# Two of four column groups of an output projection as seven block products on token rows, with weight sums made by adding transfers

## The chip, the cores and the metric

The kernel runs on one core of one Trainium2 chip. The metric is the device time of one execution in microseconds. Before the change it is 1609.59 us, the median of three runs (1609.36 to 1610.12). The profile is of one further execution, which took 1609.98 us and whose span from the first to the last instruction is 1608.3 us.

## The reference, cut to what matters

One layer of a decoder trunk: 512 tokens, width 2048, float32. What is computed last, and what the change touches, is the output projection with its gate, the residual and the final norm:

```
def rmsnorm(x, g):
    y = xf * lax.rsqrt(jnp.mean(xf * xf, axis=-1, keepdims=True) + NORM_EPS)
    return y * g
...
merged = jax.nn.sigmoid(g_mla) * y_mla + jax.nn.sigmoid(g_sgu) * y_sgu   # (512, 2048)
x = x + gate[:, None] * (merged @ w_out[l])                              # w_out (2048, 2048)
return rmsnorm(x, final_norm_g)
```

## The kernel before, in words

**Precision.** Every large product is made of float32 values split in two: a high part in the matmul's own 32-bit type (fp32r) and a low part, the rest. A product takes three matmuls, high by high, high by low, low by high (`mm3`, lines 134 to 137). A split is a ScalarE cast for the high part and a VectorE subtraction for the low part, which reads the cast's result (`hilo`, lines 139 to 141, and `Stream.split_to`, lines 105 and 106).

**The weights' stream.** `Stream` holds the list of all weight tiles of the program in the order in which they are used. A tile is 128 rows of 1024 float32, 512 KB, called a granule here. It lands in one of three raw buffers `wraw0` to `wraw2` and is split into one of two pairs, `w0h`/`w0l` or `w1h`/`w1l`. `get(i, ahead)` splits up to granule i + ahead and then asks for as many transfers as raw buffers are free. `load_before` hangs other transfers ahead of a granule's on SyncE's queue.

**The order is the order of the text.** Nothing reorders instructions: each engine takes its own in the order in which the function writes them, and waits at the first whose inputs or buffer are not ready. Work that is to happen beside a granule's matmuls is written behind the split of the next granule. `pend` is a list of such work; `get` runs one entry of it.

**The output projection.** The activations lie as `mh[j]`, `ml[j]`, 16 chunks of 128 channels by 512 tokens. They are the stationary side, 128 tokens at a time, so that tokens come to lie on the partitions of the result; the weights are the moving side, 512 columns wide. The 2048 columns are four groups `cg`. A granule (cg, i) holds chunks 2i and 2i + 1 for 512 columns; `out_granule` (line 1481) runs its 2 x 4 x 3 = 24 matmuls into four PSUM banks, one for each 128 tokens (n). Column group 0 begins inside the last attention head, while the last heads' chunks are still being made (`merge_a`, line 1451); its granules 3 to 7 and the groups 1 and 2 follow in lines 1552 to 1558. Group 3's eight granules are split into buffers of their own during group 2 (`last_tiles`), and its products run at the end token block by token block, the last block in two halves of 256 columns (lines 1564 to 1575), so that rows can be finished one after the other.

**The end of a column group.** `residual` (line 1541) is, for 128 tokens by 512 columns: VectorE multiplies the bank by the gate row (`sig<-ps,gbc`), adds x (`y<-sig,y`), ScalarE squares and sums the row (`sig<-y`, line 1548), and VectorE multiplies by the final gain (`y<-y,gfb`). For groups 0 to 2 it is put on `pend`. When a token block's last columns are in, the row sum gives a square root on ScalarE (line 1579), a reciprocal on VectorE (line 1580), a scaling in four pieces, and four stores.

## Time and profile before

| | |
|---|---|
| time, median of three runs | 1609.59 us |
| time of the profiled execution | 1609.98 us |
| its span | 1608.3 us |
| TensorE busy | 1594.2 us, 99% |
| VectorE busy | 1165.3 us, 72% |
| ScalarE busy | 755.5 us, 47% |
| GpSimd busy | 105.4 us, 7% |
| mean granted TensorE clock | 0.999 |
| first matmul of granule (0, 4) | 1446.73 us |
| last matmul begins | 1599.56 us |

Times in rows are microseconds from the span's start. In a row of the timeline stand start, duration, engine, source line, operation, what it writes and reads, and in brackets how long the engine had been idle and what ended that. A TensorE row's duration reaches beyond the start of the next, since matmuls are pipelined: the distance of the starts is what counts. Names there leave buffer numbers out: `ps` is any PSUM bank, `w0h` the high part of a split weight tile, `gbc` the gate row, `gfb` the final gain, `sig` a scratch tile, `y` the result.

### The profile page before, as it was taken

The page shows a single profiled execution, that of the slowest core. Times are in us where ns is not written, and L with a number is a line of the kernel's source. Part 1 is how long each engine was busy: PE and PEld are TensorE (multiplying, and loading weights), DVE is VectorE, ACT ScalarE, POOL GpSimd, SP SyncE. Part 2 cuts the span into 40 slices and gives each one's busy share as a digit, 9 for nine tenths or more (in the row PEclk, how much of TensorE's full clock was granted, in tenths as well). Part 3 has the DMA queues.
Part 4 walks back from the last instruction along what each step waited for, and adds up shares of the span by engine and source line. Part 5 has one row for each costly group of instructions (what it writes and reads, how often), then busy time and mean ns, then how long its engine had stood idle before and what let it go on. Part 6 is the DMA issues. An engine that isn't in the chain of part 4 may idle for free.

```text
span 1608.3 us, 26988 instructions
## 1 busy us (share of the span) xinstructions
PE 1594.2 (99%) x10760; PEld 1488.5 (93%) x10760; DVE 1165.3 (72%) x1719; ACT 755.5 (47%) x1259; POOL 105.4 (7%) x128
## 2 busy tenths in 40 slices
PE   9999999999999999999999999999999999999997
PEld 8888889999999999999999999999988889888886
DVE  8989679658777777777677777666777888763453
ACT  4443334355545454454465554554655554542322
POOL 0000000001111111111111111112000000000000
PEclk9999999999999999999999999999999999999999
DMA  9988489568899897898887998887422233336422
GB/s 379 354 296 317 171 280 324 170 193 202 219 253 252 226 252 214 233 258 212 231 253 203 250 268 207 238 193 181 162 87 88 82 105 89 90 109 227 136 87 105
DMA packets 122766, 329.64 MB, mean 205 GB/s; under 512 B 14072, under 2 KB 35600, under 8 KB 115856
## 3 DMA queue, kind: packets, MB, share of 16 engines
q1 hardware_dynamic: 104768, 269.72, 48.0%
q0 software_dynamic: 17872, 58.20, 20.8%
q8 instruction: 84, 1.38, 0.3%
q14 instruction: 42, 0.34, 0.1%
HBM read 303.95 MB, written 23.93 MB: 204 GB/s over the span
## 4 chain that ended last, share of the span: by engine, by line
PE 90%; DVE 4%; DMA 2%; ACT 1%; issue 1%; SPq 0%; DVEq 0%; ACTq 0%
PE ps L1267 15%; PE ps L1269 15%; PE ps L1268 15%; PE ps L136 14%; PE ps L137 14%; PE ps L135 14%; PE ps L1429 1%; DVE wada L126 1%; PE ps L1392 1%; PE ps L1393 1%; DVE t L123 1%; DMA wraw<-in_w 1%; DMA lat<-v_d 1%; DVE lat L123 1%; DMA rope_d<-half 0%
## 5 line engine op out<-in xcount | busy, mean ns | idle before, releaser
L106 DVE TENSOR_TENSOR w0l<-wraw,w0h 128x1024 fp32r<-128x1024 f32 (+3 forms) x74 | 78.8, 1066 | 58.8 <-ACT w0h L105 58.5
L105 ACT CAST w1h<-wraw 128x1024 fp32r<-128x1024 f32 (+3 forms) x74 | 63.9, 863 | 118.8 <-PE ps L137 57.7
L1267 PE MATMUL ps<-hh,w0h 128*128 128x256 f32 x416 | 118.5, 285 | 0.9 <-DVE lat L123 0.9
L105 ACT CAST w0h<-wraw 128x1024 fp32r<-128x1024 f32 (+3 forms) x74 | 68.9, 931 | 106.6 <-PE ps L137 66.5
L1269 PE MATMUL ps<-hh,w0l 128*128 128x256 f32 x416 | 117.7, 283 | 0.0
L1268 PE MATMUL ps<-hl,w0h 128*128 128x256 f32 x416 | 117.7, 283 | 0.0
L106 DVE TENSOR_TENSOR w1l<-wraw,w1h 128x1024 fp32r<-128x1024 f32 (+3 forms) x74 | 73.1, 988 | 59.6 <-ACT w1h L105 58.6
L1267 PE MATMUL ps<-hh,w2h 128*128 128x256 f32 x400 | 113.5, 284 | 0.0
L1267 PE MATMUL ps<-hh,w1h 128*128 128x256 f32 x400 | 113.4, 283 | 0.0
L1268 PE MATMUL ps<-hl,w1h 128*128 128x256 f32 x400 | 113.2, 283 | 0.0
L1269 PE MATMUL ps<-hh,w2l 128*128 128x256 f32 x400 | 113.2, 283 | 0.0
L1268 PE MATMUL ps<-hl,w2h 128*128 128x256 f32 x400 | 113.2, 283 | 0.0
L1269 PE MATMUL ps<-hh,w1l 128*128 128x256 f32 x400 | 113.2, 283 | 0.0
L126 DVE SCALAR_TENSOR_TENSOR wada<-wada,cact 128x2048 f32<-128x2048 f32 x47 | 107.1, 2280 | 0.0
L123 DVE TENSOR_TENSOR w2l<-raw,w2h 128x1024 fp32r<-128x1024 f32 x56 | 68.5, 1224 | 39.0 <-ACT w2h L649 38.9
L136 PE MATMUL ps<-w0l,hh 128*128 128x256 f32 (+3 forms) x288 | 92.7, 322 | 0.1
L135 PE MATMUL ps<-w0h,hh 128*128 128x256 f32 (+3 forms) x288 | 92.7, 322 | 0.0
L137 PE MATMUL ps<-w0h,hl 128*128 128x256 f32 (+3 forms) x288 | 92.4, 321 | 0.0
L135 PE MATMUL ps<-hh,w1h 128*128 128x512 f32 x226 | 89.7, 397 | 0.0
L136 PE MATMUL ps<-hl,w1h 128*128 128x512 f32 x226 | 88.3, 391 | 0.8 <-DVE hl L126 0.8
L137 PE MATMUL ps<-hh,w1l 128*128 128x512 f32 x226 | 88.1, 390 | 0.0
L629 POOL DMA_DIRECT2D wraw<-in_wh x67 | 59.2, 939 | 439.8 <-DVE w0l L123 211.7
(350 smaller groups left out, 5400.5 us busy)
## 6 DMA issues: line engine op xcount, KB each, us to landing
raw<-in_wh SPq DMA_DIRECT2D x105, 512.0 KB, 6.9
wada<-in_wada SPq DMA_DIRECT2D x47, 1024.0 KB, 7.4
wraw<-in_wh POOLq DMA_DIRECT2D x67, 512.0 KB, 6.9
wraw<-in_wh SPq DMA_DIRECT2D x45, 512.0 KB, 7.8
raw<-in_wh POOLq DMA_DIRECT2D x42, 512.0 KB, 7.8
wraw<-in_wo SPq DMA_DIRECT2D x32, 512.0 KB, 3.7
half<-in_w SPq DMA_DIRECT2D x35, 256.0 KB, 5.4
wraw<-in_w SPq DMA_DIRECT2D x16, 512.0 KB, 8.9
```

The costliest lines, as they stand in the source:

```text
L105: self.nc.scalar.copy(hi[:, :n], raw[:, :n])
L106: self.nc.vector.tensor_tensor(out=lo[:, :n], in0=raw[:, :n], in1=hi[:, :n].bitcast(F32), op=ALU.subtract)
L123: DVE.tensor_tensor(out=out, in0=in0, in1=in1, op=op)
L126: DVE.scalar_tensor_tensor(out=out, in0=in0, scalar=scalar, in1=in1, op0=op0, op1=op1, **kw)
L135: PE.matmul(ps, ah, bh, start=start, stop=False)
L136: PE.matmul(ps, ah, bl, start=False, stop=False)
L137: PE.matmul(ps, al, bh, start=False, stop=stop)
L629: q_.dma_start(t, wh[h, n, q // 10 - 1], **eng)
L1267: PE.matmul(ps, wH[:, sl], xh, start=st, stop=False, skip_group_check=True)
L1268: PE.matmul(ps, wH[:, sl], xl, start=False, stop=False, skip_group_check=True)
L1269: PE.matmul(ps, wL[:, sl], xh, start=False, stop=sp, skip_group_check=True)
L1392: PE.matmul(ps, q2[:, q], krh[:, :n], start=False, stop=False)
```

## The change

Column groups 0 and 3 stay as they were, one after the other, and come first. Groups 1 and 2 together become one 2 x 2 block product by Strassen's scheme (in the form with seven products). The blocks on the activations' side are the two halves of the tokens (`left` 0 to 255, `right` 256 to 511) by the two halves of the channels (chunks c and c + 8). On the weights' side they are the two halves of the channels by the two column groups; block 12 is first channels, column group 2.

- **Sums of activations.** `make_dsum(c)`, for c = 0 to 7, forms three sums of 128 x 256 and splits each (five VectorE operations, three casts, three subtractions). It is written behind the granules (0, 4) to (0, 7) and (3, 0) to (3, 3). `make_third(c)` forms a fourth sum over the right half of chunk c in place (two VectorE operations, one split), behind the granules of the products 1 and 7.
- **Sums of weights.** Four tiles `chain[i]` are loaded with block 11, and GpSimd's queue adds to them by adding transfers: block 12 (for product 6), block 22 (for product 2), block 21 (for product 4). Product 3's tiles are loaded with block 12 into a raw buffer, and block 22 is added to the same buffer by a transfer. The products 1, 7 and 5 use a block as it is.
- **Products.** In the order 6, 1, 7, 2, 5, 3, 4, each in four granules (p, i) of 2 chunks x 2 token blocks x 3 = 12 matmuls of 512 columns. The split of the next granule is written ahead of each granule, the work in `tasks` behind it. Product 4 comes last, one token block whole and one in two halves of 256 columns, from buffers of its own.
- **After the products.** `after(p, n2)` copies or combines banks into y, multiplies by the gate, and adds x by an adding transfer; `left_rows` finishes the 256 left tokens during product 4.

The output's tile `y` is split into `y0`, `y3` and two tiles that take over the buffers of the first sums (`s1h`, `s1l`).

**ScalarE, where the first results of the direct column groups are worked off.** Before, column group 1 (the casts of granules (1, 1) to (1, 4) with the squares of group 0 between them):

```order
L105 CAST w0h_131_16183<-wraw1_131_16091 128x1024
L1548 ACTIVATE sig_2083_16192,ssy_2076_16021<-y_2075_16020 128x512
L105 CAST w1h_132_16219<-wraw2_132_16122 128x1024
L1548 ACTIVATE sig_2085_16228,ssy_2076_16021<-y_2075_16020 128x512
L105 CAST w0h_133_16255<-wraw0_133_16153 128x1024
```

Now, column group 3 (the casts of granules (3, 1) to (3, 3); `s1h`, `s2h`, `s4h` are the high parts of the three sums):

```order
L105 CAST w0h_131_16248<-wraw1_131_16117 128x1024
L1554 ACTIVATE sig_2102_16260,ssy_2087_16032<-y0_2081_16026 128x512
L140 CAST s1h_2073_16018<-sig_2104_16288 128x256
L140 CAST s2h_2075_16020<-sig_2103_16287 128x256
L140 CAST s4h_2077_16022<-sig_2104_16288 128x256
L105 CAST w1h_132_16300<-wraw2_132_16161 128x1024
L1554 ACTIVATE sig_2106_16312,ssy_2087_16032<-y0_2081_16026 128x512
L140 CAST s1h_2073_16018<-sig_2108_16340 128x256
L140 CAST s2h_2075_16020<-sig_2107_16339 128x256
L140 CAST s4h_2077_16022<-sig_2108_16340 128x256
L105 CAST w0h_133_16352<-wraw0_133_16205 128x1024
```

Between a square and the next granule's cast stand three more casts, whose inputs VectorE makes behind the residual's last multiplication.

**VectorE, the same place.** Before, from the subtraction of granule (1, 1) to that of (1, 2):

```order
L106 TENSOR_TENSOR w0l_131_16184<-wraw1_131_16091,w0h_131_16183 128x1024
L123 TENSOR_TENSOR sig_2082_16189<-ps0_2052_15864,gbc_2073_16018 128x512
L123 TENSOR_TENSOR y_2075_16020<-sig_2082_16189,y_2075_16020 128x512
L123 TENSOR_TENSOR y_2075_16020<-y_2075_16020,gfb_2074_16019 128x512
L106 TENSOR_TENSOR w1l_132_16220<-wraw2_132_16122,w1h_132_16219 128x1024
```

Now, from that of granule (3, 1); the rows end with the three low parts, and the subtraction of (3, 2) comes next:

```order
L106 TENSOR_TENSOR w0l_131_16249<-wraw1_131_16117,w0h_131_16248 128x1024
L123 TENSOR_TENSOR sig_2101_16257<-ps0_2052_15864,gbc_2079_16024 128x512
L123 TENSOR_TENSOR y0_2081_16026<-sig_2101_16257,y0_2081_16026 128x512
L123 TENSOR_TENSOR y0_2081_16026<-y0_2081_16026,gfb_2080_16025 128x512
L123 TENSOR_TENSOR sig_2103_16287<-b4_1718_13905,g4_1719_13906 128x512
L123 TENSOR_TENSOR sig_2104_16288<-b12_1992_15513,g12_1993_15514 128x512
L123 TENSOR_TENSOR sig_2104_16288<-sig_2103_16287,sig_2104_16288 128x256
L123 TENSOR_TENSOR sig_2103_16287<-sig_2104_16288,sig_2103_16287 128x256
L123 TENSOR_TENSOR sig_2104_16288<-sig_2104_16288,sig_2103_16287 128x256
L123 TENSOR_TENSOR s1l_2074_16019<-sig_2104_16288,s1h_2073_16018 128x256
L123 TENSOR_TENSOR s2l_2076_16021<-sig_2103_16287,s2h_2075_16020 128x256
L123 TENSOR_TENSOR s4l_2078_16023<-sig_2104_16288,s4h_2077_16022 128x256
```

Eight operations have come between the residual and the next granule's subtraction.

**ScalarE in the block products,** which have no counterpart before: the casts of granules (6, 2), (6, 3), (1, 0), (1, 1) and (1, 2). `raw` is a chain tile, `y3` column group 3, `b0` the high part of the fourth sum, and the rows of line 1673 copy product 6 out of its bank:

```order
L140 CAST w1h_2128_16596<-raw2_2085_16030 128x1024
L1554 ACTIVATE sig_2131_16615,ssy_2087_16032<-y3_2082_16027 128x512
L140 CAST w0h_2132_16618<-raw3_2086_16031 128x1024
L1554 ACTIVATE sig_2135_16637,ssy_2087_16032<-y3_2082_16027 128x512
L140 CAST w1h_2136_16641<-wraw2_2117_16562 128x1024
L1554 ACTIVATE sig_2140_16662,ssy_2087_16032<-y3_2082_16027 128x512
L140 CAST w0h_2145_16672<-wraw0_2118_16564 128x1024
L140 CAST b0_1582_13103<-sig_2148_16690 128x256
L1673 COPY s1l_2142_16669<-ps0_2122_16572 128x512
L140 CAST w1h_2149_16696<-wraw1_2119_16566 128x1024
```

Between two casts there now lies one granule of 12 matmuls, where it was one of 24.

**The diff, cut to its core:**

```diff
     go = {}
-    for cg in range(3):
+    for cg in (0, 3):
         for i in range(8):
             go[cg, i] = ws.add(wo[cg, i], GW)
...
+    def w_block(q, i):
+        return wo[q % 10, (q // 10 - 1) * 4 + i]
+    def chain_load(i, q):
+        if q == 11:
+            DMA.dma_start(chain[i], w_block(q, i))
+        else:
+            nc.gpsimd.dma_start(chain[i], w_block(q, i), accum_op=ALU.add)
...
+    def make_dsum(c):
+        a, b = (nt(tp, [P, S], F32, "sig", bufs=3) for _ in range(2))
+        tt(a, mh[c].bitcast(F32), ml[c].bitcast(F32), ALU.add)
+        tt(b, mh[c + 8].bitcast(F32), ml[c + 8].bitcast(F32), ALU.add)
+        tt(b[:, right], a[:, right], b[:, right], ALU.subtract)
+        tt(a[:, left], b[:, right], a[:, left], ALU.subtract)
+        tt(b[:, left], b[:, left], a[:, left], ALU.add)
+        for n, src in (("s1", b[:, right]), ("s2", a[:, left]), ("s4", b[:, left])):
+            hilo(dsum[n + "h"][:, c], dsum[n + "l"][:, c], src)
+    def make_third(c):
+        a = nt(tp, [P, S], F32, "sig", bufs=3)
+        tt(a, mh[c].bitcast(F32), ml[c].bitcast(F32), ALU.add)
+        tt(a[:, left], a[:, left], a[:, right], ALU.subtract)
+        hilo(mh[c][:, right], ml[c][:, right], a[:, left])
+    todo = [lambda c=c: make_dsum(c) for c in range(8)]
+    for cg in (0, 3):
+        if cg:
+            pso = [bank_at(4 + k) for k in range(NB)]
+        for i in range(0 if cg else 3, 8):
+            out_granule(cg, i, pso, 0 if (cg, i) == (3, 7) else 1)
+            if (cg, i) > (0, 3) and todo:
+                todo.pop(0)()
         for n in range(NB):
-            pend.append(lambda n=n, cg=cg, ps=pso[n]: residual(n, cg, slice(cg * 512, (cg + 1) * 512), ps))
-    wl = [get(go[3, i], 0) for i in range(8)]
+            pend.append(lambda n=n, cg=cg, ps=pso[n]: residual(n, cg and 1, columns(cg), yt[cg][:, n], ps))
+    seven = (6, 1, 7, 2, 5, 3, 4)
+    block_of = {1: 11, 7: 22, 5: 21, 3: 12}
...
+    def take(p, i):
+        raw_of[p, i] = t = nt(wp, [P, GW], F32, f"wraw{n_raw[0] % 3}")
+        n_raw[0] += 1
+        DMA.dma_start(t, w_block(block_of[p], i))
+        if p == 3:
+            nc.gpsimd.dma_start(t, w_block(22, i), accum_op=ALU.add)
...
+    def add_x(half, n2, col):
+        n = 2 * half + n2
+        nc.gpsimd.dma_start(y_of(col, half, n2), xn[n][:, columns(col)], accum_op=ALU.add)
+    def after(p, n2):
+        b = banks_of(p)[n2]
+        if p == 6:
+            ACT.copy(y_of(2, 1, n2), b)
...
+        elif p == 3:
+            gated(y_of(1, 1, n2), b, 1)
+            add_x(1, n2, 1)
+            y = y_of(2, 1, n2)
+            tt(y, y, b, ALU.subtract)
+            gated(y, y, 2)
+            add_x(1, n2, 2)
...
+    for s, (p, i) in enumerate(steps):
+        if s == 0:
+            split_step(p, i)
...
+        if p == 4:
+            break
+        if steps[s + 1][0] != 4:
+            split_step(*steps[s + 1])
+            if steps[s + 1] in stream and n_take < len(stream):
+                take(*stream[n_take])
+                n_take += 1
+        granule(p, i, banks_of(p), (0, 1))
+        for f in (pend[:1] if p == 6 else []) + tasks.pop((p, i), []):
+            f()
```

More of the change, by code (lines that the diff above doesn't have):

```diff
@@ new lines, in norm_of, with finish_row @@
+    def norm_of(col, half, n2):
+        norm_part(2 * half + n2, 2 if half else col + 1, columns(col), y_of(col, half, n2), False)
+    def finish_row(n, r, pieces):
+        for k, (cols, y, kind) in enumerate(pieces):
+            if kind == "last":
+                stt(y, y, r, gfb[:, cols], ALU.mult, ALU.mult)
+            elif kind == "act":
+                ACT.activation(y, y, AF.Copy, scale=r)
+            else:
+                ts(y, y, r, None, ALU.mult)
+            DMA.dma_start(out[n][:, cols], y)
```

187 lines of the change are left out of this document (137 added, 50 removed).

## The prediction, made before the changed kernel was run

> **What bounds the kernel now.** I read the page first: who is busy, and whose work ended last.
>
> ```profile
> span 1608.3 us, 26988 instructions
> PE 1594.2 (99%) x10760; PEld 1488.5 (93%) x10760; DVE 1165.3 (72%) x1719; ACT 755.5 (47%) x1259; POOL 105.4 (7%) x128
> PE 90%; DVE 4%; DMA 2%; ACT 1%; issue 1%; SPq 0%; DVEq 0%; ACTq 0%
> ```
>
> TensorE bounds the whole program, so matmuls saved are time saved, as long as TensorE is fed. Next I looked at the busy time of each engine in the stage that changes (us, PE, PEld, DVE, ACT, POOL, granted clock, DMA share, GB/s).
>
> ```profile
> 1450.00:1500.00 50.00, 50.00 (x223) 41.39 (x221) 18.97 (x21) 12.38 (x17) 0.00 (x0) 1.00 0.53 186
> 1500.00:1550.00 50.00, 50.00 (x222) 41.42 (x221) 25.94 (x27) 18.16 (x23) 0.00 (x0) 1.00 0.48 156
> ```
>
> TensorE has no gap there, and VectorE and ScalarE have half their time free. By shares alone there is room. Whether it is usable is decided by the handover of one granule, which the timeline shows.
>
> ```profile
> 1452.17 0.39 PE L135 MATMUL ps<-w0h,b 128*128 128x512 f32 x1
> 1452.37 1.05 ACT L105 CAST w1h<-wraw 128x1024 fp32r<-128x1024 f32 x1 [4.34 <-PE ps L137]
> 1453.46 1.22 DVE L106 TENSOR_TENSOR w1l<-wraw,w1h 128x1024 fp32r<-128x1024 f32 x1 [4.17 <-ACT w1h L105]
> 1457.61 0.39 PE L135 MATMUL ps<-w1h,b 128*128 128x512 f32 x1
> ```
>
> A granule of 24 matmuls takes 1457.61 - 1452.17 = 5.44 us. The cast for the next one starts 0.20 us after the boundary, since only then is its buffer pair free; the subtraction starts 1.09 us after the cast and ends at +2.51. So there are 2.9 us of slack. In the block products a granule is half as long, 2.72 us, and the slack is 0.2 us (0.4 counting that the low part is first used by the second matmul).
>
> **What the change removes.** Column groups 1 and 2 were 2 x 8 granules, now 6 x 4 halves of one and product 4. Full-width matmuls go from 720 to 696, those of 256 columns (the last token block's) from 96 to 48. The halves' pitch comes from these two rows, 48 matmuls apart:
>
> ```profile
> 1594.12 0.42 DVE L123 TENSOR_TENSOR sig<-ps,gbc 128x256 f32<-128x256 f32 x1 [1.47 <-PE ps L137]
> 1599.88 0.42 DVE L123 TENSOR_TENSOR sig<-ps,gbc 128x256 f32<-128x256 f32 x1 [3.61 <-PE ps L137]
> ```
>
> 24 x 5.44/24 + 48 x 5.76/48 = 5.4 + 5.8 = **11.2 us less**, if TensorE stays fed.
>
> **What it adds: chains through two engines.** ScalarE takes its instructions in written order, so a cast queued behind a square or another cast waits for what that one waits for. The residual of 128 x 512 shows the chain:
>
> ```profile
> 1555.73 1.05 ACT L105 CAST w0h<-wraw 128x1024 fp32r<-128x1024 f32 x1 [4.38 <-PE ps L137]
> 1556.82 1.23 DVE L106 TENSOR_TENSOR w0l<-wraw,w0h 128x1024 fp32r<-128x1024 f32 x1 [4.22 <-ACT w0h L105]
> 1557.96 0.68 DVE L123 TENSOR_TENSOR sig<-ps,gbc 128x512 f32<-128x512 f32 x1
> 1558.68 0.69 DVE L123 TENSOR_TENSOR y<-sig,y 128x512 f32<-128x512 f32 x1
> 1559.40 0.63 ACT L1548 ACTIVATE sig<-y 128x512 f32<-128x512 f32 x1 [2.62 <-DVE y L123]
> 1559.94 0.19 ACT L1548 ACTIVATION_READ_ACCUMULATOR sig<-y 128x1 f32 x1
> 1560.16 0.69 DVE L123 TENSOR_TENSOR y<-y,gfb 128x512 f32<-128x512 f32 x1 [0.79 <-ACT sig L1548]
> 1560.77 0.68 DVE L123 TENSOR_TENSOR sig<-ps,gbc 128x512 f32<-128x512 f32 x1
> ```
>
> From the cast's start to the square's end, when ScalarE can take the next cast: 1560.13 - 1555.73 = 4.40 us. Beside granules of 5.44 us that is hidden. The sums' pieces are seen in the earlier projection, which makes the like:
>
> ```profile
> 224.83 1.28 DVE L123 TENSOR_TENSOR t<-hh,hl 128x512 f32<-128x512 f32 x2
> 226.03 0.41 DVE L123 TENSOR_TENSOR lat<-t 128x256 f32<-128x256 f32 x1
> 226.37 0.88 DVE L123 TENSOR_TENSOR t<-t,t 128x256 f32<-128x256 f32 x2
> 227.28 0.42 DVE L123 TENSOR_TENSOR lat<-t,t 128x256 f32<-128x256 f32 x1
> L140 ACT CAST s2h<-t 128x256 fp32r<-128x256 f32 x8 | 3.3, 408 | 0.3
> 1411.36 1.77 ACT L140 CAST lat<-ps 128x512 fp32r<-128x512 f32 x3
> 1413.02 0.59 ACT L140 CAST hh<-ps 128x512 fp32r<-128x512 f32 x1
> ```
>
> So 512 columns take VectorE 0.60 (0.72 when the operation needs the one before it), 256 columns 0.46 in a dependent row; ScalarE takes 0.37 (0.41 less the overlap) for 256 and 0.55 for 512 out of a bank.
>
> *Column group 0, granules 4 to 7.* Split plus `make_dsum`: 1.09 + 1.14 + 0.60 + 0.72 + 3 x 0.46 + 0.37 = 5.30 us until ScalarE is free. Under 5.44: hidden, cost nothing; 0.2 us more on each step would show.
>
> *Column group 3, granules 0 to 3.* The residual of group 0 stands in between: cast to cast is 1.09 + 1.14 + 1.44 (to the square) + 0.76 (square to last multiplication) + 0.61 + 0.60 + 0.72 + 3 x 0.46 + 0.37 = 8.1 us. Four of these from +0.2 put the fifth cast at 32.7; TensorE can start that granule 2.13 us later (subtraction's end less one matmul's pitch), at 34.8 instead of 5 x 5.44 = 27.2. **+7.6 us**; the slack of the first granule is in it.
>
> *Products 6, 1, 7.* Behind each of the four granules of product 6 hangs a residual of group 3: 4.40 us a step. Behind each of product 1 and 7 hangs `make_third`, 1.09 + 1.14 + 0.72 + 0.46 + 0.37 = 3.78 us, with a bank's copy behind it in half of them, 4.33 us. Against 2.72. The cast chain runs 0.2 + 4 x 4.40 + 4 x 4.33 + 4 x 3.78 = 50.2, so granule (2, 1) starts at 52.4 instead of 13 x 2.72 = 35.4: **+17.0 us**. Product 2 has nothing behind it (2.51 us against 2.72), so nothing is made up either.
>
> *Products 5 and 3.* VectorE has two splits in some steps, by the same rows 0.5 us in product 5 and 0.9 in product 3. The larger part is the transfers:
>
> ```profile
> DMA  9988489568899897898887998887422233336422
> wraw<-in_wh POOLq DMA_DIRECT2D x67, 512.0 KB, 6.9
> wraw<-in_wo SPq DMA_DIRECT2D x32, 512.0 KB, 3.7
> DMA to landing us min/median/max: 5.3/6.9/10.7
> DMA to landing us min/median/max: 2.5/4.3/11.8
> ```
>
> The first line is the busy share of the DMA engines in 40 slices of the span. The fourth is the adding transfers' (GpSimd queue), the fifth that of SyncE's loads. The products load 52 tiles of 512 KB where 32 were loaded, 10.5 MB more over some 150 us or 70 GB/s, which the share of 0.5 has room for; what counts is how long one takes to land. A tile of product 3 needs a load and then an adding transfer into the same buffer: 2.5 + 5.3 = 7.8 us at best, 3.7 + 6.9 = 10.6 at the medians. The buffer for (3, 0) comes free when (5, 1) is split, 2.5 us into product 5; its cast is due 8.9 us in. That leaves 6.4, so 1.4 to 4.2 are missing, less 0.3 that the cast had in hand: 1.1 to 3.9. (3, 1) and (3, 2) have used the delay; the buffer of (3, 3) frees when the delayed (3, 0) is split, and the same 1.1 to 3.9 come again. Together 1.4 + 2.2 to 7.8 = 3.6 to 9.2. The adding transfers of before ran where the DMA share was 0.8 to 0.9 (slices 10 to 28), fuller than here, which speaks for the low end; here several are asked for at once, which speaks for the high end. I take the middle, **+6.4 us**. On GpSimd's queue the additions of x stand behind the waiting ones of product 3, and on SyncE's the first stores behind the last load; neither is due before. The adding transfers into `chain` have 8 us and more of lead and cost nothing; if that cover went, their 6.9 would hold ScalarE, behind which all casts stand.
>
> [...]
>
> *The tail.* Before, a token block's chain is seen alone:
>
> ```profile
> 1588.37 0.69 DVE L123 TENSOR_TENSOR sig<-ps,gbc 128x512 f32<-128x512 f32 x1 [6.35 <-PE ps L137]
> 1591.91 0.74 DVE L126 SCALAR_TENSOR_TENSOR y<-y,ry,gfb 128x512 f32<-128x512 f32 x1
> 1594.58 0.43 DVE L123 TENSOR_TENSOR y<-sig,y 128x256 f32<-128x256 f32 x1
> 1596.12 0.15 DVE L132 TENSOR_SCALAR ry<-ry 128x1 f32<-128x1 f32 x1
> 1602.66 0.48 DVE L126 SCALAR_TENSOR_TENSOR y<-y,ry,gfb 128x256 f32<-128x256 f32 x1
> ```
>
> The last matmul is done about 1599.85 and the last operation at 1603.14: 3.3 us. Now product 4 lasts only 5.44 + 2 x 2.88 = 11.2 us, and VectorE does in that time, in order and only after product 3 (+0.2): six operations of `after(3)` (3.9 us), two `left_rows` with a square and a multiplication each (two copies, a square and the multiplication behind a root, about 3.4 us each by the same kind of rows), a block's chain (1592.65 - 1588.37 = 4.3, and 0.3 for its sum), the first half's (1596.27 - 1594.12 = 2.2) and the last (3.3). Sum 20.8 us, or 9.5 after TensorE's end instead of 3.3: 6.2 more; with the adding transfers of x landing 6 us after they are asked for, about 2 more. **+7.2 us** (6.2 to 8.2). The stores behind are as before.
>
> **Sum.** -11.2 + 7.6 + 17.0 + 6.4 + 7.2 = +27.0 us on the profiled execution's 1609.98 (its span is 1608.3, 1.7 us lie around it), so 1637.0; the median of the runs is 0.4 lower, so **1636.6 us**. About 0.2% is what a measurement of this kernel can tell from no change.
>
> **Rivals.**
> 1. *Only busy time counts, the handovers overlap: faster.* The shares of 1450 to 1550 speak for it; the 0.79 us that VectorE idles for the square in the residual's rows, and the order of the casts, speak against. Then column group 3 has 1.14 + 2.05 + 3.65 = 6.84 us of VectorE a granule (+2.5 after slack), product 6 has 3.19 (+1.5), the products 1 and 7 fit, and the tail and the transfers are hidden: -11.2 + 4.0 = -7.2, 1602.4 us. It decides from the point where a cast-to-cast chain is under 2.72 us. Chance 0.05.
> 2. *Adding transfers land like loads,* 3.7 us: each of the two delays is 0.7, the term is 2.8 instead of 6.4, 1633 us. For it: the DMA share is 0.5 here and was fuller where the 6.9 were taken. Against: 5.3 at the least. [...] Chance 0.12.
> 3. *Adding transfers land like the slowest,* 10.7 us: two delays of 7.7, the term is 16.8, 1647 us. For it: several of them at once with loads of the products. Chance 0.07.
> 4. *TensorE's clock falls in the gaps,* 1.6 us in every 4.3. The windows show it granted in full wherever matmuls run, and less only where there are none:
>
> ```profile
> 1590.00:1596.00 6.00, 6.00 (x53) 6.00 (x52) 2.97 (x8) 2.08 (x6) 0.00 (x0) 1.00 0.49 175
> 1600.00:1608.00 8.00, 0.00 (x0) 0.00 (x0) 2.17 (x6) 1.92 (x5) 0.00 (x0) 0.75 0.37 131
> ```
>
> At half clock a granule of the products takes 5.44, more than any chain: 13 x 5.44 = 70.7 instead of 52.4, 18.3 more, 1655 us. [...] Chance 0.08.
>
> **Numbers.** The forecast has 0.66, rivals 0.05, 0.12, 0.07 and 0.08, and 0.02 stay for no change. Range: the low ends of the last two terms give 1632.8, their high ends 1640.4; sixteen chain steps (four of 8.1, twelve in the products) priced 0.35 us too long or 0.4 too short, the size of the handovers in them, give 1627 and 1647. That holds rivals 2 and 3 and leaves out 1 and 4. Faster 0.05, same 0.02, slower 0.93.
>
> **What would show it.** In the changed profile: TensorE idle from granule (3, 2) on, ended by VectorE's low parts; casts 8.1 us apart in column group 3, 4.4 in product 6, 4.3 or 3.8 in 1 and 7, 2.7 in 2; casts of (3, 0) and (3, 3) waiting for an adding transfer; some 10 us between the last matmul and the last operation. Wrong, if casts stand 2.7 us apart in product 6, or TensorE's clock is below 1.00 there, or the end follows the last matmul by 4 us.

## The result, and the profile after

The changed kernel takes 1644.74 us (median of five runs, 1642.78 to 1646.35); the kernel before, beside it, 1609.59 us (five runs, 1608.82 to 1611.01). The ratio is 1.0218, with a 95% interval of 1.0203 to 1.0233: slower, 8 us above the forecast of 1636.6 and inside its range. The profiled execution took 1644.1 us with a span of 1642.3, 34.0 longer than before's.

Its page, first the lines on who is busy and the granted clock, then (with packets, MB and the share of 16 engines) the two large DMA queues. `q1` carries the plain transfers, `q0` the adding ones.

```profile
span 1642.3 us, 27103 instructions
PE 1598.1 (97%) x10688; PEld 1480.0 (90%) x10688; DVE 1219.4 (74%) x1819; ACT 783.6 (48%) x1311; POOL 125.0 (8%) x152
PEclk9999999999999999999999999999999999999997
q1 hardware_dynamic: 106064, 269.72, 47.1%
q0 software_dynamic: 21328, 68.69, 24.0%
```

VectorE and ScalarE are hardly busier than before (74 and 48% for 72 and 47%), yet the kernel lost 34 us: the loss is waiting. The stages show where it is (us, PE, PEld, DVE, ACT, POOL, granted clock, DMA share, GB/s):

```profile
1468.00:1505.00 37.00, 31.01 (x128) 23.97 (x127) 29.79 (x52) 13.66 (x27) 1.70 (x2) 0.98 0.65 172
1521.00:1540.00 19.00, 15.80 (x61) 10.86 (x59) 13.66 (x17) 7.67 (x13) 2.54 (x3) 1.00 0.72 131
1575.00:1590.00 15.00, 14.66 (x64) 11.70 (x63) 10.54 (x11) 8.06 (x9) 2.56 (x3) 1.00 0.91 209
1590.00:1605.00 15.00, 10.96 (x33) 7.27 (x32) 6.36 (x7) 3.99 (x4) 4.27 (x5) 0.77 0.99 209
```

In column group 3 (first row) and product 6 (second row) TensorE has holes while the DMA engines have room. In the products 2 and 5 (third row) it is fed. In product 3 (fourth row) it stands still for over a quarter of the time, VectorE is busy for 6.36 of 15 us, and the DMA engines are full, though they move only 209 GB/s.

**Column group 3.** ScalarE's casts of two successive granules, the square and the first sum's cast between them:

```profile
1476.31 1.05 ACT L105 CAST w1h<-wraw 128x1024 fp32r<-128x1024 f32 x1
1480.03 0.63 ACT L1554 ACTIVATE sig<-y 128x512 f32<-128x512 f32 x1 [2.67 <-DVE y L123]
1483.17 0.41 ACT L140 CAST s1h<-sig 128x256 fp32r<-128x256 f32 x1 [2.42 <-DVE sig L123]
1484.40 1.04 ACT L105 CAST w0h<-wraw 128x1024 fp32r<-128x1024 f32 x1
```

The next granule's cast comes 8.09 us after the last, as the prediction had it (8.1), and 5.1 of these are ScalarE's waits for VectorE, ahead of a cast whose own input has long been there.

**Product 6,** the same engine:

```profile
1520.97 1.05 ACT L140 CAST w0h<-raw 128x1024 fp32r<-128x1024 f32 x1 [4.39 <-PE ps L137]
1524.63 0.63 ACT L1554 ACTIVATE sig<-y 128x512 f32<-128x512 f32 x1 [2.62 <-DVE y L123]
1525.26 1.03 ACT L140 CAST w1h<-raw 128x1024 fp32r<-128x1024 f32 x1
```

4.29 us from cast to cast (predicted 4.40). Behind the granules of the products 1 and 7 they stand 4.19 us apart where a bank's copy follows and 3.71 where none does, in product 2 2.80.

**Product 3.** Its four casts, and the two later ones of its adding transfers on GpSimd's queue:

```profile
1593.78 1.04 ACT L140 CAST w1h<-wraw 128x1024 fp32r<-128x1024 f32 x1 [5.75 <-DMA wraw<-in_wo]
1599.94 1.04 ACT L140 CAST w0h<-wraw 128x1024 fp32r<-128x1024 f32 x1 [4.17 <-DMA wraw<-in_wo]
1605.61 1.04 ACT L140 CAST w1h<-wraw 128x1024 fp32r<-128x1024 f32 x1 [3.66 <-DMA wraw<-in_wo]
1608.41 1.05 ACT L140 CAST w0h<-wraw 128x1024 fp32r<-128x1024 f32 x1 [1.76 <-DMA wraw<-in_wo]
```
```profile
1599.11 0.85 POOL L1610 DMA_DIRECT2D wraw<-in_wo  x1 [7.10 <-issue]
1602.97 0.84 POOL L1610 DMA_DIRECT2D wraw<-in_wo  x1 [3.00 <-DVE s1h L123]
```

All four wait for their tile, not two of them. The tiles of the third and fourth row land 6.5 and 5.4 us after the adding transfer is asked for.

**The tail.** The last matmul, a wait for x, and the last operation:

```profile
1626.20 0.27 PE L1640 MATMUL ps<-s4h,g 128*128 128x256 f32 x1
```
```profile
1622.39 0.63 ACT L1554 ACTIVATE sig<-s1l 128x512 f32<-128x512 f32 x1 [1.35 <-DMA s1l<-in_xn]
1636.39 0.48 DVE L126 SCALAR_TENSOR_TENSOR s1l<-s1l,ry,gfb 128x256 f32<-128x256 f32 x1
```

10.4 us lie between them (1636.87 - 1626.47), where there were 3.3.

**The loss by stages.** First matmuls in the changed kernel: granule (3, 0) of column group 3 at 1467.96, (6, 0) at 1520.77, (2, 2) at 1574.73, product 4 at 1614.95. Fully fed, these stretches would take 8 x 5.44 = 43.5, 14 x 2.72 = 38.1 and 10 x 2.72 = 27.2 us. So 9.3, 15.9 and 13.0 us are lost, and 10.4 - 3.3 = 7.1 in the tail: 45.3, less the 11.2 of saved matmuls, is 34.1, where the spans differ by 34.0. The same subtraction, made on each experiment below (the tail up to the last operation of any engine):

| kernel | time, us | column group 3 | products 6, 1, 7 | products 2 (from its third granule), 5, 3 | tail over before's 3.3 |
|---|---|---|---|---|---|
| changed | 1644.7 | 9.3 | 15.9 | 13.0 | 7.1 |
| late halves | 1622.4 | 1.3 | 1.5 | 13.1 | 7.7 |
| no addition in product 3 | 1633.9 | 7.7 | 15.9 | 1.5 | 10.3 |
| no x | 1640.4 | 9.3 | 15.9 | 10.7 | 4.9 |
| sums later | 1636.1 | 0.0 | 16.0 | 12.9 | 7.5 |
| longer lead | 1620.0 | 0.0 | 2.2 | 9.9 | 9.4 |
| early x | 1617.0 | 0.0 | 2.1 | 9.9 | 6.5 |
| other tail | 1613.8 | 0.0 | 2.1 | 9.8 | 2.4 |
| adding queue | 1611.4 | 0.0 | 2.1 | 7.8 | 2.4 |
| splits later | 1614.3 | 0.0 | 2.1 | 9.7 | 3.1 |
| both | 1611.6 | 0.0 | 2.1 | 7.2 | 1.5 |
| sums on GpSimd | 1626.2 | 0.0 | 11.4 | 9.4 | 2.8 |
| sums on VectorE | 1606.1 | 0.0 | 2.0 | 3.7 | 1.4 |

Where nothing waits, ten granules of the column of the products 6, 1, 7 and two of the next take 2.81 us instead of 2.72: those whose activations are one of the first three sums. That is 0.9 and 0.2 us that no wait makes.

### The profile page after: what moved, and what is told of

Same layout as the page of the kernel before. It is cut to its first block, busy times and chain, and to the rows that moved or that the text cites. A ratio compares the mean times of both kernels' runs of the same rounds, so it can differ in the third digit from the quotient of the medians.

```text
span 1642.3 us, 27103 instructions
## 1 busy us (share of the span) xinstructions
PE 1598.1 (97%) x10688; PEld 1480.0 (90%) x10688; DVE 1219.4 (74%) x1819; ACT 783.6 (48%) x1311; POOL 125.0 (8%) x152
## 3 DMA queue, kind: packets, MB, share of 16 engines
q1 hardware_dynamic: 106064, 269.72, 47.1%
q0 software_dynamic: 21328, 68.69, 24.0%
## 5 line engine op out<-in xcount | busy, mean ns | idle before, releaser
L105 ACT CAST w0h<-wraw 128x1024 fp32r<-128x1024 f32 (+3 forms) x69 | 63.6, 922 | 87.5 <-PE ps L137 48.9
L106 DVE TENSOR_TENSOR w0l<-wraw,w0h 128x1024 fp32r<-128x1024 f32 (+3 forms) x69 | 72.7, 1054 | 41.4 <-ACT w0h L105 41.0
L105 ACT CAST w1h<-wraw 128x1024 fp32r<-128x1024 f32 (+3 forms) x69 | 58.5, 848 | 91.2 <-PE ps L137 35.9
L123 DVE TENSOR_TENSOR w1l<-wraw,w1h 128x1024 fp32r<-128x1024 f32 x51 | 62.4, 1224 | 48.4 <-ACT w1h L638 37.2
L123 DVE TENSOR_TENSOR w0l<-wraw,w0h 128x1024 fp32r<-128x1024 f32 x51 | 62.4, 1224 | 45.9 <-ACT w0h L638 37.5
L106 DVE TENSOR_TENSOR w1l<-wraw,w1h 128x1024 fp32r<-128x1024 f32 (+3 forms) x69 | 67.0, 971 | 34.7 <-ACT w1h L105 33.7
```

Of the source, the lines that this page charges most:

```text
L105: self.nc.scalar.copy(hi[:, :n], raw[:, :n])
L106: self.nc.vector.tensor_tensor(out=lo[:, :n], in0=raw[:, :n], in1=hi[:, :n].bitcast(F32), op=ALU.subtract)
L123: DVE.tensor_tensor(out=out, in0=in0, in1=in1, op=op)
```

## The experiments

The theory after the result had four parts: the order in ScalarE's queue makes the loss in column group 3 and in the products 6, 1, 7; load and adding transfer, on DMA engines that are full, the loss in the products 5 and 3; VectorE's serial work with the waits for x the tail; and a drop of TensorE's clock (0.77 granted from 1590 to 1605 us) adds a little. Rival causes stand in each expectation.

**Late halves: the same instructions in another order.**

```diff
         tt(y, t, y, ALU.add)
-        norm_part(n, part, cols, y, last)
+        later.append(lambda: norm_part(n, part, cols, y, last))
...
-            hilo(dsum[n + "h"][:, c], dsum[n + "l"][:, c], src)
+            later.append(lambda n=n, src=src: hilo(dsum[n + "h"][:, c], dsum[n + "l"][:, c], src))
...
-        hilo(mh[c][:, right], ml[c][:, right], a[:, left])
+        later.append(lambda: hilo(mh[c][:, right], ml[c][:, right], a[:, left]))
...
+        flush()
         granule(p, i, banks_of(p), (0, 1))
```

`flush` runs and empties the list `later`; in column group 3 it stands in `get`, behind the split.

> The same instructions in another order: the second half of every piece of side work (the residual's square and multiplication by the final gain, the casts and low parts of the sums of activations) is written one granule later, behind the next granule's split. Theory (the order in ScalarE's queue makes the stalls): casts stand 5.44 us apart in column group 3 up to what VectorE's 6.84 us of work a step adds, and 2.7 to 3.2 apart in the products 6, 1 and 7; the stall of column group 3 goes from 9.3 to about 3 us, that of the products 6, 1, 7 from 15.9 to about 3; the stall by the transfers of product 3 (13.0) and the tail (7.0) stay: about 1625 us (1622 to 1631). Rival (the amount of work on VectorE and ScalarE makes them): nothing changes, 1643 to 1646 us.

1622.4 us (median of 4; ratio to before 1.0084, 1.0067 to 1.0100). The same 27103 instructions, 22 us less. ScalarE in product 6 now:

```profile
1514.07 1.05 ACT L140 CAST w1h<-raw 128x1024 fp32r<-128x1024 f32 x1 [1.76 <-PE ps L1648]
1515.03 0.62 ACT L1562 ACTIVATE sig<-y 128x512 f32<-128x512 f32 x1
1516.93 1.05 ACT L140 CAST w0h<-raw 128x1024 fp32r<-128x1024 f32 x1 [1.19 <-issue]
1518.34 0.63 ACT L1562 ACTIVATE sig<-y 128x512 f32<-128x512 f32 x1 [0.36 <-DVE y L123]
```

The first square no longer waits, the second for 0.36 us instead of 2.62, and the casts stand 2.86 us apart. Column group 3 took 1511.07 - 1466.22 = 44.9 us, the products up to (2, 2) 1550.63 - 1511.07 = 39.6. So the order, not the amount of work, made 22.4 of the 25.2 us that column group 3 and the products 6, 1, 7 had lost.

**No addition in product 3.**

```diff
     DMA.dma_start(t, w_block(block_of[p], i))
-    if p == 3:
-        nc.gpsimd.dma_start(t, w_block(22, i), accum_op=ALU.add)
```

> Product 3's weights stay block 12: the adding transfers of block 22 are left out, everything else is as in the changed kernel. Theory (load and adding transfer one after the other, on crowded DMA engines, delay the splits of product 3): the stall of the products 5 and 3 goes from 13.0 to 2 to 4 us, 1634 us (1632 to 1637). Rival (VectorE's and ScalarE's double splits in these products make it): it stays at 11 or more, 1643 us.

1633.9 us, one run. Product 4 starts 1601.49 - 1572.75 = 28.7 us after (2, 2). The casts of product 3 wait for TensorE again and no longer for a tile:

```profile
1590.18 1.05 ACT L140 CAST w0h<-wraw 128x1024 fp32r<-128x1024 f32 x1 [1.42 <-PE ps L1638]
1592.85 1.06 ACT L140 CAST w1h<-wraw 128x1024 fp32r<-128x1024 f32 x1 [0.66 <-PE ps L1638]
1595.57 1.05 ACT L140 CAST w0h<-wraw 128x1024 fp32r<-128x1024 f32 x1 [1.66 <-PE ps L1638]
```

Of the 13.0 us, 11.5 hang on the four adding transfers. Of the 1.5 that stay, 1.3 are the double splits, which the prediction had at 1.4. The tail has grown by 3.2: its work starts earlier, and three of its squares wait 3.11, 2.03 and 0.79 us for x.

**No x.**

```diff
     n = 2 * half + n2
-    nc.gpsimd.dma_start(y_of(col, half, n2), xn[n][:, columns(col)], accum_op=ALU.add)
```

> The eight adding transfers of x into column groups 1 and 2 are left out (x is missing there), the rest as in the changed kernel. Theory (the DMA engines are full while product 3's weights are fetched, and x's 1 MB in that stretch is part of it): the delay of product 3 shrinks by 2 to 5 us, and the tail by 1 to 2, 1639 us (1637 to 1642). Rival (each transfer's own latency makes the delay, whatever else moves): product 3's stall stays at 12 to 13, the tail loses 0 to 1, 1643 to 1645 us.

1640.4 us, one run. From (2, 2) to product 4 1613.40 - 1575.54 = 37.9 us, 10.7 lost instead of 13.0, and the tail 4.9 instead of 7.1. Both moved as expected of full engines, but x's transfers are the small part.

**Sums later.**

```diff
-            if (cg, i) > (0, 3) and todo:
+            if i > 3 and todo:
                 todo.pop(0)()
```

> The last four sums of activations are written behind the granules 4 to 7 of column group 3, where no residual stands, instead of 0 to 3. Theory (a step of residual plus sums takes ScalarE's queue 8.1 us, one of them alone 4.4 or 5.3): the stall of column group 3 goes from 9.3 to 0 to 1 us, with the dip of the clock in it, and the rest stays, 1635.5 us (1634 to 1638). Rival (the stall belongs to the sums themselves, wherever they stand): 1643 to 1646 us.

1636.1 us, one run. Column group 3 takes 1512.28 - 1468.76 = 43.5 us, nothing lost. The sums cost nothing where no residual stands beside them; the collision of the two did.

**Longer lead.** The two orders together, and:

```diff
-    n_raw, n_part = [ws.next_raw], [ws.next_part]
+    n_raw, n_part = [0], [ws.next_part]
+    rings = [(wp, f"wraw{(ws.next_raw + q) % 3}") for q in range(3)] + [(dp[0].p, f"ex{q}") for q in range(2)]
...
-    while n_take < 3:
+    while n_take < len(rings):
```

> The late second halves and the later sums together, and two more raw buffers for the products' weights, so that product 3's loads and adding transfers are asked for five tiles ahead instead of three. Theory (product 3's stall is the time of load plus adding transfer on crowded DMA engines against too short a lead): the stall of the products 5 and 3 goes from 13.1 to 2 to 6 us, the tail stays at 7 to 8: about 1611 us (1608 to 1615). Rival (the DMA engines have no room at all there, so that asking earlier only moves the crowd): the stall stays at 10 or more, 1618 to 1621 us.

1620.0 us (4 runs; 1.0058, 1.0042 to 1.0075). My theory missed here: the stall went only to 9.9, and the rival's time came. What is late now is not product 3's tile but the chain's, for product 4, on ScalarE:

```profile
1573.28 1.04 ACT L140 CAST s2h<-raw 128x1024 fp32r<-128x1024 f32 x1 [7.35 <-DMA raw<-in_wo]
1574.23 1.04 ACT L140 CAST w1h<-wraw 128x1024 fp32r<-128x1024 f32 x1
```

That cast is not due before product 4 and holds the one behind it. The chain's additions were asked for late, since one of product 3's stood ahead of them on GpSimd's queue and waited 12.42 us there:

```profile
1563.08 0.85 POOL L1619 DMA_DIRECT2D ex<-in_wo  x1 [12.42 <-DVE s1h L123]
1563.62 2.94 POOL L1547 DMA_DIRECT2D raw<-in_wo  x3
```

So two more causes were possible, the two queues, beside full engines.

**Early x.**

```diff
         if p == 6:
-            ACT.copy(y_of(2, 1, n2), b)
+            gated(y_of(2, 1, n2), b, 2)
+            add_x(1, n2, 2)
         elif p == 1:
-            ACT.copy(y_of(1, 0, n2), b)
+            gated(y_of(1, 0, n2), b, 1)
+            add_x(0, n2, 1)
...
+        task(1, 2 + n2, lambda n2: DMA.dma_start(y_of(1, 1, n2), xn[2 + n2][:, columns(1)]), n2)
```

> As with the longer lead, and x goes earlier: the copies of product 6 and product 1 are gated at once and x is added to them then, the right tokens' column group 1 gets x by plain loads, and four of the fourth sums move to product 2. Only two of eight adding transfers of x stay where they were. Theory (the transfers of x crowd product 3's and hold the tail's squares): the stall of the products 5 and 3 goes to 1 to 4 us, the tail to 5 to 6, though VectorE gets two more operations there: about 1608 us (1605 to 1612). Rival (the tail is VectorE's serial work alone): tail 8 to 9, no gain over the longer lead alone, 1611 us.

1617.0 us (4 runs; 1.0041, 1.0026 to 1.0056), above both expectations, since the stall stays at 9.9. The tail is 6.5, between the two, instead of 9.4, with two VectorE operations more, so the waits for x had held it: none of its squares waits for x any longer.

**Other tail.**

```diff
-            tt(y, y, gfb[:, cols], ALU.mult)
+            (eng or DVE).tensor_tensor(out=y, in0=y, in1=gfb[:, cols], op=ALU.mult)
...
-        norm_part(2 * half + n2, 2 if half else col + 1, columns(col), y_of(col, half, n2), False)
+        norm_part(2 * half + n2, 2 if half else col + 1, columns(col), y_of(col, half, n2), False, nc.gpsimd if half else None)
...
-                          for cg, k in ((0, "act"), (1, "act"), (2, "dve"), (3, "dve"))])
+                              for cg, k in ((0, "act"), (1, "act"), (2, "pool"), (3, "pool"))])
```

> As with the early x, and in the tail some of VectorE's work goes to GpSimd and ScalarE: the multiplication of the right tokens' column group 2 by the final gain, half of the scaling of the left rows, and one piece of each last row; both left blocks' sums, roots and reciprocals are written side by side. Theory (VectorE's 22 us of serial work behind product 3 against 11 us of product 4 make the tail): about 5 us of VectorE's work less, tail 2 to 4 us over before's, 1604 us (1601 to 1608). Rival (GpSimd and VectorE hold each other up, or the adding transfers still set the end): tail at 5 or more, 1607 to 1611 us.

1613.8 us (10 runs; 1.0025, 1.0016 to 1.0035). The tail came as expected (2.4). The time fits neither expectation, since both had counted on a smaller stall, and it is still 9.8.

**Adding queue, splits later, both.** The first writes product 3's additions one granule behind their loads, the second moves product 4's splits back, the third does both and orders the tail's VectorE work anew:

```diff
-            nc.gpsimd.dma_start(t, w_block(22, i), accum_op=ALU.add)
+            adds.append(lambda: nc.gpsimd.dma_start(t, w_block(22, i), accum_op=ALU.add))
...
-    for i, at_ in enumerate(((5, 1), (5, 2), (5, 3), (3, 0))):
+    for i, at_ in enumerate(((5, 3), (3, 0), (3, 1), (3, 2))):
```

> As the kernel with the other tail, with one thing changed: product 3's adding transfers are written one granule after their loads, so that the chain's additions of block 21 do not stand behind them in GpSimd's queue. Theory (the first of product 3's adding transfers waits 10 us for its own load and holds the three additions into the chain behind it, for which ScalarE's early casts of product 4's weights wait): those three are asked for about 8 us earlier, and the stall of the products 5 and 3 goes from 9.8 to 2 to 5 us, 1608 us (1606 to 1611). Rival (the DMA engines are full there, whatever the order): the stall stays at 8 or more, 1612 to 1615 us.

> As the kernel with the other tail, with one thing changed: product 4's splits stand two granules later, so that their casts wait less for the chain's additions and hold the products' casts behind them less. Theory (a cast that is not due yet waits in ScalarE's queue ahead of one that is): the wait of 8.0 us for the chain's second tile shrinks by two granules, 5.4 us, and the stall of the products 5 and 3 goes from 9.8 to 3 to 6 us, 1609 us (1607 to 1612). Rival (full DMA engines: product 3's own tiles are as late): the stall stays at 8 or more, 1612 to 1615 us.

> Both changes of the queues, and the tail's VectorE work in another order: the last block's second half is gated before the first half is finished, two pieces of the left rows are scaled while VectorE waits for a root, one after the block's stores, GpSimd scales only two pieces. Theory: stall of the products 5 and 3 at 1 to 3 us, tail 0.5 to 2 us over before's 3.3, the products 6, 1 and 7 at 2.5: 1603 us (1600 to 1607), faster than before. Rival (full DMA engines): 1610 to 1614 us, not faster than before.

1611.4 and 1614.3 us (one run each) and 1611.6 (11 runs; 1.0011, 1.0002 to 1.0020). With the other order on GpSimd's queue the chain's additions are asked for at 1550 instead of 1562 us, but the stall falls only from 9.8 to 7.8; with the later splits it does not fall. With both, ScalarE waits for product 3's own tile again. In the third kernel:

```profile
1572.58 1.04 ACT L140 CAST w0h<-ex 128x1024 fp32r<-128x1024 f32 x1 [4.81 <-DMA ex<-in_wo]
1576.95 1.05 ACT L140 CAST w1h<-ex 128x1024 fp32r<-128x1024 f32 x1 [2.38 <-DMA ex<-in_wo]
```
```profile
1560.00:1580.00 20.00, 16.73 (x66) 12.80 (x65) 13.18 (x16) 8.58 (x9) 4.38 (x5) 0.91 1.02 228
1580.00:1590.00 10.00, 9.14 (x39) 6.90 (x38) 9.40 (x13) 4.69 (x11) 0.00 (x0) 1.00 0.00 0
```

The DMA share is 1.02 for 20 us and then nothing: whatever order the transfers take, the last lands when all are done. The rival of all three, full engines, came true or nearly so (7.8 where it had 8 or more); the order of the queues made 2 us of the stall. The third kernel's tail is the shortest up to then, but its stores bunch behind it: the span ends 7.2 us after the last operation (1609.7 - 1602.47), where it is 5.2 in the kernel before.

**Sums on GpSimd.** The blocks 22 and 21 are in the raw tiles of the products 7 and 5 anyway:

```diff
         hilo(hi, lo, raw)
+        if p in (7, 5):
+            nc.gpsimd.tensor_tensor(out=chain[i], in0=chain[i], in1=raw, op=ALU.add)
...
-        task(6, min(i + 2, 3), chain_load, i, 22)
-        task(2, min(i + 2, 3), chain_load, i, 21)
```

> As the kernel with both changes of the queues, but blocks 22 and 21 are added into the chain by GpSimd itself, from the raw tiles that the products 7 and 5 load anyway, so that eight of the twelve adding transfers of weights in the products are gone; the multiplications by the final gain of column group 3 and of the left rows go to GpSimd too, product 5's results are worked off one to two granules later, and the left rows' roots are taken ahead of VectorE's work on product 3. Theory (between the products 2 and 3 the DMA engines are full: 4.7 MB by adding transfers in some 25 us): the DMA share there falls to 0.5 to 0.7, the stall of the products 5 and 3 goes from 7.2 to 0 to 2 us, the product 6 loses 1, the end with its stores 1 to 3: 1603 us (1599 to 1606), faster than before. Rival (GpSimd's operations hold VectorE's up, or are themselves late for the splits of the products 2 and 4): new stalls of 4 us and more in the products 7 to 3, 1608 to 1614 us.

1626.2 us (4 runs; 1.0105, 1.0088 to 1.0122). The DMA engines did become freer (from granule (2, 2) to product 4 a share of 0.52, where the kernel with both has 0.85), but the rival's mechanism came, and cost more than its 1608 to 1614 us. Two additions on GpSimd, and a low part on VectorE beside them:

```profile
1530.08 2.71 POOL L1636 TENSOR_TENSOR raw<-raw,ex 128x1024 f32<-128x1024 f32 x1
1532.42 2.65 POOL L1636 TENSOR_TENSOR raw<-raw,wraw 128x1024 f32<-128x1024 f32 x1
```
```profile
1530.19 5.97 DVE L123 TENSOR_TENSOR w0l<-ex,w0h 128x1024 fp32r<-128x1024 f32 x1 [0.98 <-ACT w0h L140]
1536.09 0.68 DVE L123 TENSOR_TENSOR sig<-b,g 128x512 f32<-128x512 f32 x1
```

The subtraction takes 5.97 us instead of 1.23: it ends 1.1 us after the second addition (1536.16 and 1535.07), TensorE waits 4.21 us for it, and its clock is at 0.50 for 6.8 us behind that (0.83 in the mean from 1530 to 1550). The products 6, 1 and 7 lose 11.4 us instead of 2.1. In product 2 the same happens, and granule (2, 2) takes 8.47 us instead of 2.81:

```profile
1558.96 4.97 POOL L1636 TENSOR_TENSOR raw<-raw,ex 128x1024 f32<-128x1024 f32 x2
1559.13 5.10 DVE L123 TENSOR_TENSOR sig<-sig 128x256 f32<-128x256 f32 x1
```

So the 9.4 us of the next column are no stall by transfers: 5.7 are this stop with the clock at 0.50 for 3.4 us behind it, most of the rest two later ones (3.61 and 2.64 us on VectorE). Of product 3's casts only the last still waits for its tile (1.75 us). With the engines freer, the tiles were there.

**Sums on VectorE.** Only block 21, in product 2, where VectorE had room once the fourth sums had left it:

```diff
-        task(2, min(i + 2, 3), chain_load, i, 21)
+        task(2, i, lambda i: tt(chain[i], chain[i], raw_of[5, i], ALU.add), i)
...
+            for c in {(3, 1): (0,), (3, 2): (1,), (3, 3): (2, 3)}.get((cg, i), ()):
+                make_third(c)
```

> As the kernel with both changes of the queues, but only block 21 comes into the chain without a transfer, by four VectorE additions in product 2 from product 5's raw tiles; to make room, four of the fourth sums stand in column group 3 and product 5's results and the norm's pieces are spread over product 3. GpSimd keeps only the four multiplications by the final gain beside product 6; the left rows' roots are taken ahead of product 3's results. Theory (full DMA engines between the products 2 and 3 make the stall, and VectorE waits for GpSimd where both work from SBUF): four adding transfers, 2.1 MB, are gone from there, the stall of the products 5 and 3 goes from 7.2 to 1 to 4 us, no VectorE operation of the products 1 to 3 takes longer than 1.3 us, the end with its stores loses 1 to 3: 1604 us (1601 to 1608), faster than before. Rival (product 3's load and adding transfer are too long for their lead even on freer engines, or VectorE has become the bound there): the stall stays at 5 or more, 1608 to 1613 us.

1606.05 us (10 runs) against 1609.66 (14 runs): 0.9977, 0.9968 to 0.9987. It beats both kernels, by 38.7 and 3.6 us.

```profile
PE 1585.1 (99%) x10688; PEld 1476.8 (92%) x10688; DVE 1224.2 (76%) x1822; ACT 780.7 (49%) x1309; POOL 125.5 (8%) x150
PEclk9999999999999999999999999999999999999999
```
```profile
1530.00:1550.00 20.00, 20.00 (x86) 16.24 (x87) 16.30 (x23) 8.44 (x12) 2.57 (x3) 1.00 1.06 284
1560.00:1580.00 20.00, 18.14 (x76) 13.76 (x75) 15.14 (x17) 11.11 (x15) 4.32 (x5) 1.00 0.78 166
```

With four adding transfers fewer the share from 1560 to 1580 is 0.78 instead of 1.02, and the stall 3.7 instead of 7.2. What stays of it is still the transfers': three casts of product 3 wait 1.82, 3.22 and 1.23 us for their tiles. The first row shows that full engines alone do no harm: at 1.06 TensorE is fed, since nothing that moves there is due. VectorE holds more work than in the changed kernel (1224.2 us for 1219.4). One expectation failed: a low part in product 1 took 2.12 us, beside a multiplication left on GpSimd. This kernel bundles several edits, so the shares of the single ones in its last 5.5 us are not separated.

## Why the prediction was right, point by point

| step | predicted | measured |
|---|---|---|
| matmuls saved | -11.2 | not by itself; with -11.2 the sum closes to 0.1 |
| column group 3 | +7.6 | +9.3 |
| products 6, 1, 7 | +17.0 | +15.9 |
| products 5 and 3 | +6.4 (3.6 to 9.2) | +13.0 |
| tail | +7.2 | +7.1 |
| sum | +27.0 | +34.1 |

That the measured time lies in the range is in part luck. The range was made wide for the price of the chain steps, which came out right; the term that failed left its own range. By the high ends of the last two terms alone the range would have ended at 1640.4.

**Column group 3: right, and 1.7 us short.** The 8.1 us of the chain are there, and the sums-later kernel shows that the collision is all of it. Of the 1.7 us too much, the clock is the cause as far as the traces go: in the kernel without the addition in product 3, whose text is the same up to there, the stage lost 7.7. Both have a dip of the granted clock, the changed kernel at granule (3, 5), after the last of the long steps, where nothing covers it; the other one step earlier, inside a wait that ScalarE's chain makes anyway. The changed kernel's lasts from 1503.35 to 1506.76, 3.41 us at 0.50 with the matmuls 0.43 us apart instead of 0.23, by which TensorE does an estimated 1.7 us less (half of 3.41). The changed kernel:

```profile
1504.00:1508.00 4.00, 4.00 (x13) 3.17 (x12) 0.02 (x1) 0.00 (x0) 0.00 (x0) 0.65 0.80 254
1524.00:1528.00 4.00, 3.24 (x14) 2.24 (x14) 2.96 (x4) 1.66 (x3) 0.56 (x2) 1.00 0.73 116
```

The other one:

```profile
1496.00:1500.00 4.00, 4.00 (x14) 3.23 (x13) 3.31 (x7) 1.47 (x5) 0.00 (x0) 0.71 0.26 100
1504.00:1508.00 4.00, 4.00 (x19) 3.29 (x19) 0.00 (x0) 0.00 (x0) 0.00 (x0) 1.00 0.69 240
```

**Products 6, 1, 7: right.** 4.29, 4.19 and 3.71 us were predicted as 4.40, 4.33 and 3.78. That the order makes it was argued from the rows; the late halves show it.

**Products 5 and 3: the step that failed is the size of this term,** 6.4 where 13.0 were measured. The double splits were right (1.4; 1.3). What failed is "(3, 1) and (3, 2) have used the delay": all four tiles were late, and the starts of their granules stand 3.6, 3.4, 2.9 and 2.4 us further apart than 2.72. (Some 1.5 us of the last distance are the clock's, as said below.) The reason is the sentence before it, that 70 GB/s more are what "the share of 0.5 has room for". That counted bytes. In the page's queue lines q0 has 24.0% of 1642.3 us for 68.69 MB, 5.7 us a MB; q1 has 47.1% for 269.72 MB, 2.9. An adding transfer takes the engines twice as long, 3.0 us for 512 KB instead of 1.5, and eight of them with x's and the loads fall into one stretch. That it is the engines, the runs that took transfers off them show: without x's transfers the stall is 2.3 us smaller, and with the sums on GpSimd only one of product 3's four casts waits for its tile, 1.75 us. Before's page had the same two lines (20.8% of 1608.3 us for 58.20 MB, 48.0% for 269.72: 5.7 and 2.9 us a MB), so this could have been read beforehand. The third rival gave nearly the measured time (1647) by another way, two transfers of 10.7 us; the traces show four delays on full engines instead, and the second rival's 3.7 us for an adding transfer did not occur in product 3, where its two later ones took 6.5 and 5.4 us.

**The tail: right in size, and only in part for the reason given.** VectorE's serial work makes most of it (with part of it on other engines the tail fell from 6.5 to 2.4); the waits for x make 2.2 (no x: 4.9), where "about 2" were put.

**The clock, the fourth rival: right in a small part.** Beside the dip above it was 0.50 from 1595.5 to 1602.3 us, behind a gap of 3.20, where TensorE had to wait for a tile anyway, and again in product 3:

```profile
1609.20:1612.50 3.30, 3.30 (x9) 2.55 (x9) 3.04 (x5) 2.12 (x7) 0.84 (x1) 0.50 0.44 65
```

There the fourth tile's low part was ready at 1610.7, and TensorE, whose matmuls stood 0.43 us apart instead of 0.23, came to it at 1611.9: some 1.5 us. So the clock made about 3.2 of the 45.3 us lost (and, worked out the same way, some 1.6 of the stall of 9.8 with the other tail, where the clock is 0.66 from 1570 to 1580). But in the products 6, 1 and 7, which the rival was about, it stayed at 1.00 with gaps of 0.5 to 0.6 and of 1.3 us, or one of 1.0 to 1.2, in every granule that waited.

**The first rival, only busy time counts, was wrong for this order of the text and right for the work:** with the instructions in another order, column group 3 and the products 6, 1 and 7 lose 2.8 us together, where this rival had 4.0.

## What to carry to other kernels

Before work is put beside a stage that is to be shortened, write down each engine's queue for one step and look for an instruction that waits for another engine ahead of one that is due: putting the second half of such a piece of work one step later moved 22 us here without an instruction less. Judge room on the DMA engines by their busy share, with each kind of transfer at its own time per byte (here 5.7 us a MB for an adding one and 2.9 for a plain one) and stretch by stretch, not by bytes over the whole stage. Where the engines are full over the whole lead, a longer lead or another queue order helps little (3.2 and 2.0 us of 13 here); taking transfers out helps more (11.5 without product 3's additions, which the result needs, and 3.5, beside other edits, in the last kernel).

## What was not expected of the hardware

- An adding transfer took the DMA engines 5.7 us a MB, a plain one 2.9, by the queue lines of before's page (5.75 and 2.86) and of the changed kernel's (5.74 and 2.87).
- Beside GpSimd's additions, in the kernel with the sums on GpSimd, VectorE operations with their inputs in SBUF took longer: low parts of 128 x 1024 took 5.97 us beside two additions of 2.7 us, 3.65 and 3.61 beside one, instead of 1.2. Four gatings of a bank, with an input in PSUM, did not: in the same kernel the one at 1517.6 us, beside GpSimd's multiplication of 1517.5 to 1518.9, and the three at 1520.5, 1523.3 and 1526.2, beside multiplications of 1.46, took their usual 0.68. The additions of x behind the first three, with both inputs in SBUF, took 1.07 instead of 0.69; a low part beside four later multiplications (1595.8 us) took 1.29.
- TensorE's clock fell to 0.50 for 3.41 us in column group 3 (0.65 in the row of 4 us above) though no gap before it, from start to start of two matmuls, was longer than 1.72 us. What its falls in the changed kernel have in common is TensorE's busy share of the stretch before. In that trace the changes of the clock stand 3.41, 88.75, 6.83, 6.83, 3.41 and 17.07 us apart, whole multiples of 3.41. Cut at this step, up to the last matmul, and with 0.227 us counted for a matmul of 512 columns, 0.12 for one of 256 and the other widths in proportion, the trace has 470 stretches at full clock. It fell behind the three with TensorE at work for 0.07, 0.23 and 0.38 of the time, and behind none of the other 467, of which the lowest has 0.48. Before's trace has 466, none under 0.68, and no fall ahead of the last matmul. The three rows show the stretch ahead of the fall in column group 3 (0.23 by this count), the fall, and a stretch at the boundary of the products 6 and 1 (0.56). Their busy times are larger, since a row counts some 0.39 us for a matmul.

```profile
1499.94:1503.35 3.41, 1.32 (x5) 0.56 (x4) 3.00 (x6) 2.58 (x4) 0.00 (x0) 1.00 0.00 0
1503.40:1506.70 3.30, 3.30 (x10) 2.56 (x9) 0.62 (x1) 0.00 (x0) 0.00 (x0) 0.50 0.79 233
1534.07:1537.48 3.41, 2.47 (x10) 1.47 (x9) 3.09 (x4) 0.79 (x2) 0.00 (x0) 1.00 0.92 162
```

In column group 3 two waits of a granule, of 1.72 and 1.26 us, stand side by side in that stretch; in the products 6 and 1 they are 0.6 and 1.3. No run tests by itself whether the share decides.

- Twelve matmuls with one of the first three sums of activations on the stationary side take 2.81 us instead of 2.72, fully fed. With the fourth sum, which lies in the place of the activations, they take 2.72 (product 3 in the kernel without the addition). So it is not that they are sums; no run separates what else it is.
